# Attention's queries by seven block products in a stage of their own, in a one-core encoder block

## The chip, the cores and the metric

The kernel runs on one core of one Trainium2 chip. The metric is the device time of one execution in microseconds (us). TensorE (PE) multiplies matrices into PSUM (8 banks of 128 x 512 fp32), VectorE (DVE) and ScalarE (ACT) work on SBUF and PSUM, GpSimd (POOL) on SBUF alone. Transfers are started from SyncE's queue (SP), ScalarE's or GpSimd's; those from GpSimd can add into their destination. An engine works through its instructions in the order in which they are written down, and waits at each one until its inputs are there.

## The reference

One layer over T = 1040 positions (16 learned ones ahead of 1024), 1024 channels:

```
u = rms_norm(h);  z = u @ w_in                       # 7680 columns, cut into ten parts
o_r = bidirectional_retention(rot(rq), rot(rk), rv)  # 4 heads, chunks of 128, group norm
y_r = (o_r * silu(rg)) @ w_rb
o_a = windowed_attention(rot(aq), rot(ak), av, sink) # 8 heads in 2 groups, +-128 positions
y_a = (o_a * silu(ag)) @ w_ab
out = (sigmoid(gr) * y_r + sigmoid(ga) * y_a) @ w_o
return (h + rms_norm(out))[:, 16:]
```

The change is about aq = u @ w_in[aq], 1024 channels (8 heads of 128), and its rotation; and about which of the gates rg, ag, gr, ga are partly made early.

## The kernel before, in words

**Number format.** Every fp32 product is made of three matmuls in a faster format (mm3, lines 74 to 79): each operand is split into a high part h (a rounding copy, on ScalarE or GpSimd) and a low part l = value - h (dve_lo, line 91, on VectorE), and ah*bh + al*bh + ah*bl is accumulated in a PSUM bank. The input x, transposed and scaled by the norm's weights, lies in SBUF all the time as high and low part in two tiles named big (128 x 8 blocks x 1040).

**Stages.** (1) Setup, and a first projection. (2) Retention, head by head (retention): a forward pass over 9 chunks, then a backward pass over 8. The next head's query and key projection (gen_qk) is cut into steps of one mm3 per 128 channels and laid into the backward pass as a filler (fill(KT), 8 steps at a time); some gate products made ahead (gen_pre) follow. In the last head the filler is the first key group (gen_ak(0)), gate products and the first two query products (gen_aq(0, 0)). (3) The values' projection (gen_av, nine chunks). (4) Attention: 4 head pairs times 8 chunks of 128 queries. (5) The block phases z (gates), r, a (the two branch projections) and o (output projection).

**Seven products.** In the block phases a unit of 256 weight columns is taken as a 2 x 2 matrix of blocks (A11 to A22; 512 input channels by 128 columns) against x as a 2 x 2 matrix of blocks (B11 to B22; 512 channels by 512 positions). Seven products of sums of blocks, not eight of blocks, give the unit's four results (line 933 has the list: products 1 and 2 use A11*B11 and A12*B21, 3 uses B22, and 4, 5, 6, 7 use the sums T4, T1, T2, T3 of blocks of x). A product is 4 mm3 of 512 columns. T1 to T4 need space beside x; T1 takes the place of B12 in big, the last quarter of T4 that of the 16 learned positions. Phase.prepare forms and splits the weights' sums six products ahead (LEAD, line 1121); Phase.product multiplies; Phase.combine adds the results out of the PSUM banks; a post function finishes each result.

**The queries.** gen_aq (line 690) makes them the plain way: for each of 4 units, 2 column halves and 2 position halves, 8 mm3 of 512 columns. rope_late (line 180) rotates a result: two VectorE products out of PSUM (lines 184, 185), then two adding transfers from GpSimd's queue (line 187). split_q (line 661) splits it at a later step. Except for gen_aq(0, 0) all of it is filler in the attention.

**Attention.** For each chunk stage1 makes two score blocks, VectorE adds the mask and reduces (line 1423), ScalarE takes the exponential (line 1426), VectorE the reciprocal of the sum (line 1430), GpSimd scales (line 1439); stage2 transposes the weights (lines 1455 to 1460) and splits them; stage3 multiplies with the values (lines 76 to 78 and 1490). stage1 runs one chunk ahead. FILL (line 27) says how many filler steps a chunk gets, BEGUN (line 1547) what is done beside which filler step: weight fetches and splits, query splits, the sums of x for T1 to T4 (sum_fetch, sum_row), gates made ahead. tc.issue_after and follow lay an engine's instructions behind a named one; otherwise a planner orders each engine's instructions by its own estimate of when they are ready, and by their order in the program.

**Gates made ahead.** PRE (line 28) names, for gate units 2 to 13, the products whose x block is unchanged (2, and from unit 6 on 3); gen_pre makes them, stores them in DRAM (e_d), and the z phase adds them. So 20 of the z phase's 112 products are made earlier. Its first two units have an order of their own (early) that puts off T2 to T4, whose sums are read back from DRAM and split at its start (get_sum, line 1138).

Of the kernel before, what the change touches and what calls it, by code (L numbers as in the profile page):

```python
# [14 lines left out]
NM = 16  # L15
# [11 lines left out]
FILL = (9, 9, 7, 7, 7, 7, 6, 6), (7,) * 8, (7, 6, 6, 6, 6, 6, 6, 5), (5, 5, 5, 5, 5, 5, 8)  # L27
PRE = {u: (2, 3) if u > 5 else (2,) for u in range(2, 14)}
# [11 lines left out]
def block_kernel(ctx: ExitStack, tc: tile.TileContext, x0, xT, x, meta, w_in, w_rb, w_ab, w_out, post_w,  # L40
# [14 lines left out]
    def bank(tag, name):  # L55
# [12 lines left out]
    xs_d = [dram.tile([4, P, 2, 512], F32, tag=f"xs{i}", name=f"xs{i}") for i in range(2)]  # L68
    pre_d = {n: [dram.tile([P, 4, 512], F32, tag=f"pre{n}{s}", name=f"pre{n}{s}") for s in range(2)]
             for n in ("T1", "T2", "T3", "T4")}  # L70
# [354 lines left out]
    vah = va.tile([P, NB, 256], R, name="vah")  # L425
    vm = va.tile([P, 256], R, name="vm")
    vmt = va.tile([NM, 256], F32, name="vmt")
# [30 lines left out]
    def retention(h, fill, begin=lambda: None):  # L458
# [102 lines left out]
        for c in range(9):  # L561
# [7 lines left out]
            if h == NH - 1 and c == 1:  # L569
                pre_fetch(6)  # L570
            if h == NH - 1 and c == 2:
                with tc.issue_after(state["vl"]):
                    pre_sums(6)
# [10 lines left out]
            if h == 1 and c == 2:  # L584
                row_factors()
            stage2(c)
# [19 lines left out]
        for c in range(NB, 0, -1):  # L606
# [52 lines left out]
    aq, aqs, wq = {}, {}, {}  # L659

    def split_q(hp, e_, i):

        o = aq[hp][e_, i].rearrange("p (t q) -> p t q", q=64)
        if (hp, i) not in aqs:
            aqs[hp, i] = [aw.tile([P, 1024], R, tag=f"aq{t}", bufs=2, name=f"aq{t}{hp}_{i}") for t in "hl"], set()
            if len(aqs) == 1:
                aw.tile([P, 48], F32, name="space_aq")
        h, l = (t.rearrange("p (t e q) -> p t e q", e=2, q=64)[:, :, e_] for t in aqs[hp, i][0])
        nc.scalar.copy(h, o)
        dve_lo(l, o, h)  # L670
        aqs[hp, i][1].add(e_)


    def fetch_aq(hp):
        raw = fetch_w(w_in, U_AQ + hp)
        split, wq[hp] = halves_w(U_AQ + hp)
        begun["q", hp] = lambda s: split(raw[s], True)

    def fetch_ak():
        raw = fetch_w(w_in, U_AK)  # L680
        split, w_ = halves_w(U_AK)
        wak.append(w_)
        begun["k", 1] = lambda s: split(raw[s], True)

    def half_w(which, i, s):
        begun[which, i](s)

    begun = {}

    def gen_aq(hp, i, es=(0, 1)):  # L690
        if not i:
            if hp not in wq:
                wq[hp] = load_w(w_in, U_AQ + hp)
            aq[hp] = {}
        a, b = HALVES[i]
        for e_ in es:
            t = yield from proj(wq[hp], P * e_, a, b, f"paq{hp}_{i}{e_}")
            o = ra.tile([P, 512], F32, tag="q", bufs=6, name=f"aq{hp}_{i}{e_}")
            rope_late(t, a, b, o, f"aq{hp}_{i}{e_}")
            aq[hp][e_, i] = o  # L700
            yield
# [20 lines left out]
    def gen_ak(g, pieces_=range(4)):  # L722
        if not wak:
            wak.append(load_w(w_in, U_AK))
        for i in pieces_:
            a, b = PIECES[i]
# [3 lines left out]
            if not g and i:  # L730
                keys(g, i - 1)
            yield

    def last_keys():
# [3 lines left out]

    SUMS = ("T1", (0, 0), (0, 1), (0, 0)), ("T3", (0, 1), (1, 1), (0, 1)), ("T2", (1, 1), (1, 1), (0, 0)), (
        "T4", (1, 0), (1, 0), (1, 1))  # L740

    def sum_fetch(q):

        k, c = q // 2, slice(256 * (q % 2), 256 * (q % 2) + 256)
        for i in range(2):
            xsum[i] = t = ap.tile([P, 2, 256], F32, tag="xs", bufs=2, name=f"xs{i}{q}")
            nc.sync.dma_start(t, xT[4 * i + k, :, NM:T].rearrange("p (j t) -> p j t", j=2)[:, :, c])

    def sum_row(q, part):

        k, c = q // 2, slice(256 * (q % 2), 256 * (q % 2) + 256)
        if not part:
            for i, t in xsum.items():
                nc.scalar.activation(t, t, AF.Copy, scale=vec[:, 4 * i + k:4 * i + k + 1])
        x = {(i, j): t[:, j] for i, t in xsum.items() for j in range(2)}
        for _, o, a, b in SUMS[2 * part:2 * part + 2]:
            nc.vector.tensor_tensor(x[o], x[a], x[b], ALU.subtract)
        if part:
            for i, t in xsum.items():
                last["xs"] = nc.sync.dma_start(xs_d[i][k][:, :, c], t).ins  # L760

    xsum = {}
# [8 lines left out]
    def pre_split(k, i, behind):  # L771

        n, o, a, b = SUMS[i]
# [14 lines left out]
    def pre_fetch(u):  # L788
        n = P * len(PRE[u])
# [892 lines left out]
```

## Time and profile before

| | |
|---|---|
| median of 3 runs | 1041.22 us (1040.29 to 1041.6) |
| profiled execution | 1040.1 us, its span 1038.3 us |
| granted clock of TensorE | 0.999 |
| busy: TensorE, VectorE, ScalarE, GpSimd | 99%, 80%, 48%, 22% |
| TensorE instructions | 5883 matmuls, transposes included |
| query products (paq) | 384 matmuls, first at 288 us, last at 496 us |
| scores to last attention output | 332 to 550 us |
| z phase's products (bz) | 1104 matmuls, 546 to 803 us |
| moved by transfers | 188 MB, 181 GB/s on average |

The span is the time from the first to the last instruction; the execution's own time has 1.8 us more around it. A row of instructions reads: line, engine, operation, output<-inputs by tile names, shapes, count, then busy time in us and mean ns of one, then the engine's idle time just before them and what ended it. Matmuls overlap, so their shown durations add up to more than the time they take. A row of stage windows has the window, its length, each engine's busy us with the number of instructions, the granted clock, the transfer engines' share and GB/s.

### The profile page before, as it was taken

How to read it: one execution, taken by the hardware profiler on the slowest of the kernel's cores; microseconds unless marked ns; L12 is line 12 of the kernel's file. 1: busy time of each engine (PE TensorE's matmuls, PEld its weight loads, DVE VectorE, ACT ScalarE, POOL GpSimd, SP SyncE). 2: the span in 40 equal slices, each digit the busy share in tenths (PEclk: the TensorE clock that was granted, in tenths of full speed). 3: DMA queues.
4: the chain of work that ended last, by engine and by line, in shares of the span. 5: the costliest groups of instructions: out<-in, count | busy, mean ns of one | idle time of the engine just before them, and what ended most of it. 6: DMA issues, size and time to landing. Idle time of an engine off the chain costs nothing. (4 is left out here: it accounts for less than half of the span.)

```text
span 1038.3 us, 17311 instructions
## 1 busy us (share of the span) xinstructions
PE 1023.7 (99%) x5883; PEld 898.0 (86%) x5883; DVE 835.8 (80%) x1802; ACT 502.6 (48%) x1129; POOL 228.0 (22%) x368
## 2 busy tenths in 40 slices
PE   9999999999999999999999999999999999999997
PEld 8998999989989888988888888878888788788886
DVE  7886758768875778778769989999899799778665
ACT  5531432423424566665667554455567446334442
POOL 3445244243342333444310000000000000111032
PEclk9999999999999999999999999999999999999999
DMA  9433123243241466675559679899935746789464
GB/s 357 164 87 88 65 47 84 78 88 104 78 93 62 103 182 189 175 188 161 168 176 326 209 260 338 294 330 365 373 102 178 252 153 226 231 231 325 127 122 81
DMA packets 98840, 188.45 MB, mean 181 GB/s; under 512 B 13024, under 2 KB 37632, under 8 KB 98192
## 3 DMA queue, kind: packets, MB, share of 16 engines
q1 hardware_dynamic: 81200, 162.89, 46.6%
q0 software_dynamic: 10176, 14.73, 9.6%
q10 hardware_dynamic: 7376, 9.73, 2.7%
q8 instruction: 46, 0.75, 0.3%
q14 instruction: 42, 0.34, 0.1%
HBM read 124.32 MB, written 57.68 MB: 175 GB/s over the span
## 5 line engine op out<-in xcount | busy, mean ns | idle before, releaser
L1286 POOL DMA_DIRECT2D mx_d<-c1a x4 | 3.6, 890 | 395.8 <-DVE c1a L1277 377.2
L77 PE MATMUL bz<-big,llz 128*128 128x512 f32 x192 | 74.8, 390 | 0.2 <-DVE llz L92 0.2
L78 PE MATMUL bz<-big,lhz 128*128 128x512 f32 x192 | 74.4, 389 | 0.0
L76 PE MATMUL bz<-big,lhz 128*128 128x512 f32 x192 | 74.0, 390 | 0.3 <-ACT lhz L978 0.3
L76 PE MATMUL pv<-wh,big 128*128 128x256 f32 x256 | 72.8, 284 | 0.0
L77 PE MATMUL pv<-wh,big 128*128 128x256 f32 x256 | 72.7, 284 | 0.0
L78 PE MATMUL pv<-wl,big 128*128 128x256 f32 x256 | 72.7, 284 | 0.0
L76 PE MATMUL bz<-T,lhz 128*128 128x512 f32 x176 | 68.1, 390 | 1.1 <-DVE u2z L1068 1.1
L78 PE MATMUL bz<-T,lhz 128*128 128x512 f32 x176 | 68.5, 389 | 0.0
L77 PE MATMUL bz<-T,llz 128*128 128x512 f32 x176 | 68.5, 389 | 0.0
L76 PE MATMUL paq<-big,wh 128*128 128x512 f32 x128 | 51.6, 403 | 0.0
L1426 ACT ACTIVATE p<-raw,nm 128x337 f32<-128x337 f32 (+1 forms) x64 | 35.5, 556 | 32.2 <-DVE nm L1423 30.6
L77 PE MATMUL paq<-big,wl 128*128 128x512 f32 x128 | 50.2, 392 | 0.0
L78 PE MATMUL paq<-big,wh 128*128 128x512 f32 x128 | 50.2, 392 | 0.0
L1439 POOL TENSOR_SCALAR p<-p,den 128x336 f32<-128x336 f32 (+2 forms) x60 | 34.6, 624 | 66.5 <-DVE den L1430 59.1
L76 PEld LDWEIGHTS pv<-wh,big 128*128 128x128 f32 x256 | 48.3, 189 | 0.4
L77 PEld LDWEIGHTS pv<-wh,big 128*128 128x128 f32 x256 | 48.3, 189 | 0.4
L78 PEld LDWEIGHTS pv<-wl,big 128*128 128x128 f32 x256 | 48.2, 188 | 0.3
L92 DVE TENSOR_TENSOR wl<-wr,wh 128x1024 fp32r<-128x1024 f32 x28 | 35.1, 1258 | 10.4 <-POOL wh L89 6.7
L76 PEld LDWEIGHTS bz<-big,lhz 128*128 128x128 f32 x192 | 36.1, 188 | 8.1 <-ACT lhz L978 0.7
L77 PEld LDWEIGHTS bz<-big,llz 128*128 128x128 f32 x192 | 36.0, 188 | 7.9 <-DVE llz L92 0.5
L78 PEld LDWEIGHTS bz<-big,lhz 128*128 128x128 f32 x192 | 36.0, 188 | 7.5
(621 smaller groups left out, 3594.6 us busy)
## 6 DMA issues: line engine op xcount, KB each, us to landing
wrz<-in_w_in_dram SPq DMA_DIRECT2D x32, 512.0 KB, 6.1
wr<-in_w_in_dram SPq DMA_DIRECT2D x29, 512.0 KB, 4.1
we<-in_w_in_dram SPq DMA_DIRECT2D x16, 512.0 KB, 4.3
tg<-tg_d SPq DMA_DIRECT2D x32, 256.0 KB, 5.1
e<-e ACTq DMA_DIRECT2D x20, 256.0 KB, 2.7
e<-e SPq DMA_DIRECT2D x20, 256.0 KB, 5.3
xn<-in_x_dram SPq DMA_DIRECT2D x8, 512.0 KB, 9.5
oTr_d<-ost SPq DMA_DIRECT2D x16, 256.0 KB, 2.1
```

The source lines that it names most:

```text
L76: nc.tensor.matmul(o, ah, bh, start=first, stop=False, **kw)
L77: nc.tensor.matmul(o, al, bh, start=False, stop=False, **kw)
L78: latest[:] = [nc.tensor.matmul(o, ah, bl, start=False, stop=last, **kw).ins]
L92: return nc.vector.tensor_tensor(o, i, hi.bitcast(F32), ALU.subtract).ins
L1286: nc.gpsimd.dma_start(d, to, accum_op=ALU.add)
L1426: last["exp"] = nc.scalar.activation(pp[:, x_, w0 - o:w0 - o + 1 + wid], r[:, 0:1 + wid], AF.Exp, scale=-1.0, bias=nm_[:, x_:x_ + 1], accu ...
L1439: nc.gpsimd.tensor_scalar(v, v, den[:, x_:x_ + 1], 1.0, op0=ALU.mult, op1=ALU.mult)
```

## The change

- The queries get a stage of their own between the values and the attention: four units of 256 columns, each by seven block products, all eight PSUM banks. It needs T1 to T4 of x, so these are now made during the retention (row_sums, eight steps for each of four rows of blocks, one step at a chunk), split there, and stored in DRAM as high and low parts (xt_d). At the start of the query stage they are loaded in final form; T1 and T2 stay for the z phase, T3 and T4 are loaded again for it.
- A query result is rotated, split and stored in DRAM at once (q_post), from ScalarE's queue. The attention loads a head pair's half at a time (fetch_aq).
- At the two seams small pools hold what is needed first: the first products' weight parts lie in the rotation's buffers (m), the others in pools over retention's early buffers (qa, qt, qb); the attention's queries and gate operands lie in four pools in a row (aq, ep) over the place of T3.
- The second key group is made in the last retention head, in the place of the first queries, and waits in DRAM (ak_d). The values' low parts are put into DRAM during the query stage (val_d) and fetched back.
- The attention's filler is now the gates' products 5, 2 and 3 of units 8 to 15 alone (gen_gate): 96 steps, three for each chunk. Scores are made two chunks ahead, not one, with three weight buffers. GpSimd makes the gate operands' high parts (gate_part).
- The z phase runs its first two units in the usual order, and takes products 5, 2 and 3 of units 8 to 15 and product 2 of units 2 to 7 as made: 30 of 112. The sum for its product 6 comes from DRAM (s2_d). The next phase's operands are loaded and split from 25 products before its end on, not 16.

The core of the diff:

```diff
-FILL = (9, 9, 7, 7, 7, 7, 6, 6), (7,) * 8, (7, 6, 6, 6, 6, 6, 6, 5), (5, 5, 5, 5, 5, 5, 8)
-PRE = {u: (2, 3) if u > 5 else (2,) for u in range(2, 14)}
+PRE = {u: (2,) if u < 8 else (5, 2, 3) for u in range(2, 16)}
...
+    def row_sums(k):
+
+        x = va.tile([P, 2, 2, 512], F32, tag="vah", bufs=1, name=f"xs{k}")
+        with follow(asked[0]):
+            for i in range(2):
+                nc.sync.dma_start(x[:, i], xT[4 * i + k, :, NM:T].rearrange("p (j t) -> p j t", j=2))
+        yield
+        for i in range(2):
+            for j in range(2):
+                nc.scalar.activation(x[:, i, j], x[:, i, j], AF.Copy, scale=vec[:, 4 * i + k:4 * i + k + 1])
+            yield
...
+        def split(n):
+            o = x[:, *SUMS[n][0]]
+            h = va.tile([P, 512], R, tag="vm", bufs=1, name=f"xh{n}{k}")
+            nc.scalar.copy(h, o)
+            nc.sync.dma_start(xt_d[n][0][:, k], h.bitcast(F32))
+            with tc.issue_after(sums_at[0]):
+                dve_lo(o.bitcast(R), o, h)
+            nc.sync.dma_start(xt_d[n][1][:, k], o)
+
+        for ns, n in ((("T1", "T3"), None), ((), "T3"), (("T2",), "T1"), (("T4",), "T2"), ((), "T4")):
+            for m in ns:
+                minus(m)
+            if n:
+                split(n)
+            yield
...
     def retention(h, fill, begin=lambda: None):
...
+            if c > 1 and sums_at[0]:
+                sums_at[0] = state["vl"]
+                next(sums, None)
             stage2(c)
...
+            sums_at[0] = near
+            if h or c < 8:
+                next(sums, None)
...
+    def fetch_aq(n):
+
+        hp, i = n // 2, n % 2
+        aqs[hp, i] = [aqp[i].tile([P, 1024], R, tag=f"aq{t}", bufs=1, name=f"aq{t}{hp}_{i}") for t in "hl"]
+        for e_ in range(2):
+            for t, d in zip(aqs[hp, i], aq_d[hp, e_, i]):
+                nc.sync.dma_start(t.bitcast(F32).rearrange("p (t e q) -> p t e q", e=2, q=64)[:, :, e_],
+                                  d.rearrange("p (t q) -> p t q", q=64))
...
-                 [gen_ak(0), pieces(pre, 8), last_keys(), gen_aq(0, 0)])
+                 [gen_ak(0), pieces(pre, 8), last_keys(), gen_ak(1)])
...
+    def gate_part(u, p):
+
+        a11, a21, a12, a22 = (t[:, :, P * i:P * i + P] for t in raw[u] for i in range(2))
+        g = nc.vector.tensor_tensor
+        if p == 5:
+            g(a21, a21, a22, ALU.add)
+        if p == 3:
+            g(a11, a21, a11, ALU.subtract)
+            nc.sync.dma_start(s2_d[u], a11)
+            g(a22, a12, a11, ALU.subtract)
+        src = {5: a21, 2: a12, 3: a22}[p]
+        m = (3 * (u - 8) + (5, 2, 3).index(p)) // 2 % 2
+        h, l = (epp[m].tile([P, 4, P], R, tag=f"e{x_}", bufs=2, name=f"e{x_}{u}_{p}") for x_ in "hl")
+        pool_hi(h, src)
+        dve_lo(l, src, h)
+        parts[u, p] = h, l
...
+    def q_post(u, i, j, o, to=None):
+        to = o if to is None else to
+        a, b = HALVES[j]
+        rope_late(o, a, b, to, f"aq{u}_{i}{j}")
+        h = ra.tile([P, 512], R, tag="m", bufs=4, name=f"aqh{u}_{i}{j}")
+        nc.scalar.copy(h, to)
+        nc.scalar.dma_start(aq_d[u, i, j][0], h.bitcast(F32))
+        dve_lo(to.bitcast(R), to, h)
+        nc.scalar.dma_start(aq_d[u, i, j][1], to)
...
+    free[:] = ["pj"] * 3 + ["p1"] * 2 + ["p2"] * 2 + ["p3"]
+    q_seq = [(0, 1), (0, 2), (1, 1), (1, 2)] + [(e_, p) for p in (5, 6, 7, 3, 4) for e_ in range(2)]
+    q_seq += [(2 + e_, p) for p in (1, 2, 5, 6, 7, 3, 4) for e_ in range(2)]
+    q_steps = run([(Phase("q", q_seq, w_loader(w_in, range(U_AQ, U_AQ + 4)), q_post), None)])
+    next(q_steps)
+    with follow(*raw_asked):
+        for n in ("T1", "T2", "T3", "T4"):
+            get_pre(n, xt_d)
+    for _ in q_steps:
+        pass
+    free[:] = ["pj"] * 3
+    for i, t in enumerate(val):
+        val[i] = ra.tile([P, 512], R, tag="q", bufs=6, name=f"val{i}b")
+        nc.sync.dma_start(val[i].bitcast(F32), val_d[i])
...
         for k, (hp, n) in enumerate(chunks):
             ends = k >= len(chunks) - 2
-            if k + 1 < len(chunks):
+            if k + 2 < len(chunks):
                 with follow(*latest, *marks("oa", "lo")):
-                    stage1(*chunks[k + 1])
+                    stage1(*chunks[k + 2])
+                with follow(*latest):
+                    fill(1)
...
             with follow(*latest, *marks("exp", "sum")) if not ends else ExitStack():
                 stage2(hp, n)
             if not ends:
                 with follow(*latest):
-                    fill(FILL[hp][n] if k else 1)
+                    fill(2)
```

More of the change, by code (lines that the diff above doesn't have):

```diff
@@ L657, in filler @@
         return fill, drain
[L659 to L701, printed above, removed]
+    aqs = {}
+    def fetch_aq(n):
[5 more added lines that the diff above has]
+                                  d.rearrange("p (t q) -> p t q", q=64))
     kT = {}
@@ new lines, in gen_pre @@
+    def gen_pre(u):
+        t = keep.tile([P, 4, 256], F32, tag="wr", bufs=2, name=f"we{u}")[:, :, 0:P]
+        nc.sync.dma_start(t, w_in[gates[u], :, 4:8, 0:P])
+        h, l = (wp.tile([P, 4, 256], R, tag=f"w{x_}", bufs=4, name=f"we{x_}{u}")[:, :, 0:P] for x_ in "hl")
+        nc.scalar.copy(h, t)
+        dve_lo(l, t, h)
+        b = pj(f"pe{u}")
+        for k in range(4):
+            mm3(b, h[:, k], l[:, k], xh[4 + k][:, NM:NM + 512], xl[4 + k][:, NM:NM + 512], k == 0, k == 3, True)
+            if k < 3:
+                yield
+        made(u, 2, b)
+        yield
@@ L1006, in prepare @@
                 g(t, t, self.block(u, "A11"), sub)
+            elif p == 6 and 3 in known:
+                t = half("S2")
+                nc.sync.dma_start(t, s2_d[u])
+                self.split(u, 6, t)
             elif p == 6:
@@ L1361, in block_kernel @@
     ph_o = Phase("o", seq, o_load, o_post, apart=(0, 1))
[L1362 to L1363 removed]
+    steps = run([(Phase("z", sequence(16), w_loader(w_in, gates, PRE), z_post, z_fetch, late=(0, 1), pre=PRE),
                   act_src(oTr_d)),
```

408 lines of the change are left out of this document (197 added, 211 removed).

## The prediction, made before the result was known

> **What bounds the kernel now.** I read the page's busy times first, then stage windows, then the waits of TensorE, then single timelines.
>
> ```profile
> span 1038.3 us, 17311 instructions
> PE 1023.7 (99%) x5883; PEld 898.0 (86%) x5883; DVE 835.8 (80%) x1802; ACT 502.6 (48%) x1129; POOL 228.0 (22%) x368
> ```
> ```profile
> core 0: us, PE busy (x) PEld busy (x) DVE busy (x) ACT busy (x) POOL busy (x), PEclk, DMA share, GB/s
> 66.00:290.00 224.00, 224.00 (x1691) 212.46 (x1690) 168.44 (x453) 74.85 (x219) 90.35 (x136) 1.00 0.33 83
> 331.00:545.00 214.00, 211.65 (x1276) 187.56 (x1275) 161.82 (x426) 129.99 (x351) 74.21 (x156) 1.00 0.59 164
> 545.00:797.00 252.00, 250.41 (x1111) 206.76 (x1110) 234.27 (x387) 142.80 (x255) 0.00 (x0) 1.00 0.81 279
> 700.00:750.00 50.00, 50.00 (x222) 41.37 (x221) 43.09 (x70) 26.48 (x46) 0.00 (x0) 1.00 1.03 375
> ```
> ```profile
> PE idle L313 <- DVE warm L207: 1.4, 1, 1.4
> PE bz L76 <- DVE u2z L1068: 1.1, 1, 1.1
> ```
>
> TensorE is never idle in the retention (66 to 290 us), idle 2.35 us of 214 in the attention and 1.6 us of 252 in the z phase. Its longest wait is 1.4 us, at the start. So nothing but fewer matmuls can shorten this kernel by much, and every new wait of TensorE lengthens it. VectorE is the runner-up: 75% in the retention, 76% in the attention, 93% in the z phase, and at 93% TensorE lost only those 1.6 us.
>
> **What a matmul costs.** Matmuls overlap, so a price is a distance between starts.
>
> ```profile
> 401.37 0.40 PE L77 MATMUL paq<-big,wl 128*128 128x512 f32 x1
> ...
> 405.73 0.40 PE L78 MATMUL paq<-big,wh 128*128 128x512 f32 x1
> ```
> ```profile
> 0.00:1038.00 1038.00, 252.17 (x1104) 206.95 (x1104) 42.16 (x62) 23.30 (x40) 1.00 0.59 182
> ```
>
> The first fence is the start and end of twenty query matmuls in a row in the attention: 19 steps in 4.36 us, 0.2295 us each, though each is shown with 0.40 us. The second is the z phase's block products alone (tile bz, over the whole run): 1104 matmuls of the same shape in 252.17 us, 0.2284 us each. By the shown durations a dropped matmul would seem to be worth 0.39 us; that would nearly double the gain.
>
> [...]
>
> **The change, part by part.**
>
> *Matmuls.* Now: 4 weight units, 2 column halves, 2 token halves, 8 blocks, 3 matmuls: 384. After: 4 units, 7 products, 4 blocks, 3: 336. That removes 48 x 0.2295 = 11.0 us, and the other 336 run at the z phase's pace, 336 x 0.0011 = 0.4 us. The gates' products stay 112 in all: 20 were made ahead, now 30, so the z phase has 82 instead of 92. The second key group moves from the attention into the last retention head, in the place of the first queries. Their numbers don't change. **Gain 11.4 us.**
>
> *Attention's old waits.* Its 2.35 us of idle time belong to a schedule that goes. I take them off (2.3) and cost the new schedule whole.
>
> *Sums in the retention.* Each of four rows now brings 4 scalings and 4 high copies on ScalarE, 4 subtractions and 4 low parts on VectorE, 8 stores and 2 loads on SP's queue. The z row gives 234.27 us for 387 VectorE instructions, mostly of this shape: 0.605 us each. 32 of them are 19.4 us; VectorE goes from 75% to 84% of the stage. Nothing is queued behind the new instructions but the scan itself (state update, its split, the next state product). Bounds: 0, if they fall in idle time, and 19.4, if each delays the scan in full; no gain, since it only adds work. The nearest row is the z phase, 93% with 1.6 us lost: I take **1 us**.
>
> *Seam from values to queries.* The first four products use B11 and B21, which lie ready, and their weight parts use an early pool. A product is 12 x 0.2284 = 2.74 us, so T1 has 11.0 us from the stage's start, T2 16.4, T3 21.9.
>
> ```profile
> T<-preT SPq DMA_DIRECT2D x4, 1024.0 KB, 8.8
> aq<-m_aq POOLq DMA_DIRECT2D x32, 128.0 KB, 4.0
> ```
>
> A pair of such loads lands in 8.8 us. T1 overwrites x, so it can't start before the last value chunk has read its first four blocks, half a chunk ahead of the stage. It is then about 3 us early. On SP's queue the last value store and two units' weights stand ahead of it, T2 to T4 behind it at up to 375 GB/s (window 700 to 750): 2 MB each 5.6 us, as fast as pairs of products use them. Bounds 0 and 8.8 us (nothing overlaps); I take **1 us**.
>
> *The query stage.* VectorE per unit: 7 low parts, 4 sums of weights, 3 additions, and for each of 4 results two rotary products and one low part: 26, so 104 in all, 104 x 0.605 = 63 us beside 28 x 2.74 = 76.7 us of TensorE. ScalarE has 14 copies a unit. Both fit. What is new is the order: each of 16 results goes VectorE, two accumulating transfers from POOL's queue (4.0 us to land), ScalarE's copy, VectorE's low part, two stores from ScalarE's queue. If a low part stands in VectorE's queue before its transfer has landed, the next product's weight parts are queued behind it. The stores' waits hold only ScalarE, which is half idle. Operands are made six products (16 us) ahead, which hides single waits. Bounds: 0, and 16 x 4.0 - 13.7 (VectorE's spare time) = 50 us. Before, the same parts were made at a hand-set later step, so the trace doesn't show the case; nearest is again the z phase's 1.6 us: **1.5 us**.
>
> *Seam from queries to attention.* The first query pair comes back from DRAM when T3 is done with, four products (11 us) before the end; the values come back into the products' own buffers; the gate operands need T3's place too. The first softmax has four filler steps and two score products to hide in. Bounds: 0, and 9 us (four loads at 4.0 to 5 us, then a 4 us softmax, all bare); **1 us**.
>
> *The attention.* It loses most of its filler: three steps a chunk instead of about seven, with scores made two chunks ahead.
>
> ```profile
> 405.96 0.28 PE L76 MATMUL po<-pah,vah 128*128 128x256 f32 x1
> ...
> 406.77 0.32 PE L76 MATMUL ps<-kTh,aqh 128*128 128x336 f32 x1
> ...
> 407.43 0.57 DVE L1423 CUSTOM_DVE_ANT_0 raw<-ps,mask,nsink 128x336 f32<-128x336 f32 x1
> ...
> 407.69 0.60 PE L1455 MATMUL pt<-ident,p 128*128 128x128 f32 x4
> ...
> 408.37 0.47 PE L76 MATMUL paq<-big,wh 128*128 128x512 f32 x1
> ...
> 408.69 0.39 PE L77 MATMUL paq<-big,wl 128*128 128x512 f32 x1
> ...
> 409.37 0.17 DVE L1430 RECIPROCAL den<-den 128x2 f32<-128x2 f32 x1 [0.87 <-ACT p L1426]
> ...
> 411.59 1.22 DVE L92 TENSOR_TENSOR wl<-wr,wh 128x1024 fp32r<-128x1024 f32 x1
> ```
>
> TensorE: scores 406.77 to 407.69, 0.92; transposes to 408.37, 0.68; output 0.81 for a chunk of 7 matmuls, so 1.16 for the usual 10; filler 9 x 0.2295 = 2.07, and 0.09 more after the transposes (408.37 to 408.69). Together 4.92 us. VectorE: from the first score reduction (407.43) to where it is free again (411.59) 4.16 us, 0.87 of it waiting for ScalarE's exponentials; plus 48 gate instructions over 32 chunks, 1.5 x 0.605 = 0.91: 5.07 us if none falls into a wait. So the chunk is bound by TensorE by 0.76 us without gates, or by VectorE by 0.15 us with all of them serial: 0 to 4.8 us over 32 chunks. If ScalarE's copies of gate results (three in four chunks) also come ahead of the copy that VectorE waits for:
>
> ```profile
> L835 ACT COPY e<-pe 128x512 f32<-128x512 f32 x20 | 11.7, 588 | 18.4 <-PE pe L78 17.8 <-DMA wrz<-in_w_in_dram 0.6
> ```
>
> 0.75 x 0.588 = 0.44 more a chunk, up to 18.9 us in all. Most gate low parts wait for POOL's high part and can slip into the 0.87: I take **2 us**.
>
> *The z phase.* It drops 16 splits of x sums at its start and recomputes no fourth sum; T1, T2 lie ready, T3 and T4 have eight products to come. Per product it has no more VectorE work than before, so its 1.6 us stay and I cost it at nothing; without that cover T3's 8.8 us would lie open.
>
> **Sum.** The profiled execution took 1040.1 us (span 1038.3). 1040.1 - 11.4 - 2.3 + 1.0 + 1.0 + 1.5 + 1.0 + 2.0 = 1032.9. The median shown is 1.1 above the profiled execution, and I carry that over: **1034.0 us**, 0.7% less.
>
> **Rivals.**
>
> *All covers hold.* No new wait: 1040.1 - 13.7 + 1.1 = 1027.5, up to 1029.5. For it: TensorE loses nothing in the retention at 75% VectorE. Against it: three new seams. Chance 0.20.
>
> *T1 comes late.* If 3 MB stand ahead of it (8 us at 375 GB/s), TensorE waits 4 to 6 us instead of 1: about 1039. Chance 0.07. [...]
>
> *The attention becomes VectorE's.* The chain serial with ScalarE's copies in it: 9 to 18.9 us instead of 2, 1041 to 1051, nearer the first since the waits take up some. For it: 5.07 against 4.92. Against it: 0.87 us of waits in each chunk that gate parts can use. Chance 0.11; a third of it slower.
>
> *VectorE waits for the rotary transfers (slower).* The place is the low part behind the accumulating transfer in the query stage. Its price is 16 w - 13.7 for a wait of w each; it outweighs the whole saving from 16 w - 13.7 > 8.7, w > 1.4 us. With half the transfer's 4.0 us, w = 2: 18.3 us instead of 1.5, 1050.8. For it: weights, sums, queries and rotary parts are some 24 MB in 77 us, 313 GB/s, close to the 375 at which the engines are full, so transfers lengthen. Against it: 16 us of lead. Chance 0.15.
>
> **Chances.** Forecast (1029.5 to 1039) 0.47. A measurement here can tell about 0.2%: faster is below 1039.1, slower above 1043.3. Faster: 0.47 + 0.20 + 0.05 (T1 late but small) + 0.01 = 0.73. Same: 0.02 + 0.06 = 0.08. Slower: 0.04 + 0.15 = 0.19. Range: from 1027, no new wait, to 1045, which leaves most of the last rival and half of the slow attention out, near 0.2.
>
> **What would show it.** 5835 matmul instructions instead of 5883. Query products at 0.228 us from start to start over some 77 us without a break. In the waits of TensorE: under 2 us each by T1, by query operands and by attention transposes. VectorE near 84% in the retention with TensorE still full. Attention chunks of 4.9 to 5.0 us. I am wrong if query operands' low parts end TensorE's waits for over 5 us, if chunks take 5.2 us or more, or if a gap of over 3 us stands at a seam.

## The result and the profile after

The changed kernel takes **1107.06 us** (median of 4 runs, 1106.21 to 1109.97), the kernel before 1041.08 (4 runs, 1040.29 to 1041.6). The ratio is 1.064, with a 95% interval from 1.0619 to 1.066. The forecast was 1034.0 us with a range up to 1045, so it was wrong in its sign and by 73 us. The profiled execution took 1107.45 us, its span 1105.7.

The page of the changed kernel: busy time and share of each engine with its number of instructions, then two rows of the 40 slices (27.6 us each).

```profile
span 1105.7 us, 17586 instructions
...
PE 1032.2 (93%) x5835; PEld 898.0 (81%) x5835; DVE 841.4 (76%) x1812; ACT 501.0 (45%) x1133; POOL 246.7 (22%) x394
...
PE   9899999999999967449999999999999999999997
...
PEclk9999999999999997869999999999999999999999
```

The matmuls are the 5835 of the forecast. TensorE's busy time has gone up although 48 matmuls are gone: where the granted clock is low, each takes longer (a 128x512 matmul is shown with 0.63 us from 421.50 to 426 us, with 0.39 from 428.50 on). Both dips stand in slices 15 to 18, 387 to 498 us.

TensorE's three longest waits in the changed kernel (line waited for, then total, number, longest):

```profile
PE pe L79 <- ACT e L779: 23.8, 1, 23.8
PE bq L79 <- ACT u2q L1080: 15.4, 2, 15.2
PE ps L79 <- DVE nm L1482: 7.2, 4, 2.6
```

Before, the longest was 1.4 us. The two long ones name ScalarE, an engine that is busy 45% of the time. Its stages, by window:

```profile
core 0: us, PE busy (x) PEld busy (x) DVE busy (x) ACT busy (x) POOL busy (x), PEclk, DMA share, GB/s
66.00:290.00 224.00, 220.17 (x1652) 206.96 (x1651) 174.83 (x469) 88.72 (x245) 86.79 (x126) 1.00 0.45 127
345.00:440.00 95.00, 79.58 (x336) 64.51 (x336) 55.78 (x98) 27.66 (x48) 17.77 (x22) 0.91 0.76 227
440.00:490.00 50.00, 18.98 (x87) 15.35 (x86) 24.46 (x56) 13.61 (x35) 18.21 (x31) 0.73 0.75 200
```

In the query stage (345 to 440 us) and at attention's start (440 to 490) no engine is full: TensorE 84% and 38%, VectorE 59% and 49%, ScalarE 29% and 27%, the transfers 76% and 75%. Where nothing is full on average, the order of the steps is the first suspect. The retention has 39 matmuls fewer in its window than before (1652 against 1691).

The stages' lengths in us, each from the start of its first matmul (values pav, queries bq, scores ps, gates bz) in the profiled executions, with three of the experiments beside them (before, the values are followed by the attention at once):

| | before | after | e2 | c1 | c2 |
|---|---|---|---|---|---|
| start to values | 301.4 | 315.9 | 316.5 | 309.0 | 309.6 |
| values | 30.4 | 28.9 | 29.3 | 29.1 | 30.0 |
| query stage | - | 95.3 | 78.0 | 78.5 | 77.8 |
| attention | 214.2 | 194.0 | 175.6 | 181.7 | 174.0 |
| z phase to the end | 492.3 | 471.6 | 471.4 | 471.7 | 472.0 |

**The chain in the query stage.** Timelines of the changed kernel from 402 us on (start, length, and in brackets the idle time just before and what ended it): VectorE, GpSimd's queue, ScalarE.

```profile
402.02 0.69 DVE L188 TENSOR_TENSOR u2q<-u2q,cr 128x512 f32<-128x512 f32 x1
...
404.29 0.69 DVE L187 TENSOR_TENSOR m_aq<-u2q,sr 128x512 f32<-128x512 f32 x1
410.05 0.69 DVE L95 TENSOR_TENSOR u2q<-u2q,aqh 128x512 fp32r<-128x512 f32 x1 [5.07 <-ACT aqh L1398]
410.66 0.68 DVE L188 TENSOR_TENSOR u2q<-u2q,cr 128x512 f32<-128x512 f32 x1
```
```profile
403.00 1.64 POOL L190 DMA_DIRECT2D u2q<-m_aq  x2 [4.41 <-DVE u2q L188]
411.64 1.64 POOL L190 DMA_DIRECT2D u2q<-m_aq  x2 [7.00 <-DVE u2q L188]
```
```profile
409.40 0.62 ACT L1398 CAST aqh<-u2q 128x512 fp32r<-128x512 f32 x1 [5.75 <-DMA u2q<-m_aq]
...
415.48 0.62 ACT L1398 CAST aqh<-u2q 128x512 fp32r<-128x512 f32 x1 [4.94 <-DMA u2q<-m_aq]
...
419.75 0.62 ACT L1398 CAST aqh<-c5q 128x512 fp32r<-128x512 f32 x1 [3.66 <-DMA c5q<-m_aq]
420.28 0.58 ACT L1080 COPY u2q<-bq 128x512 f32<-128x512 f32 x1
```

On VectorE the sine product of post i+1 (404.29) stands ahead of post i's low part (410.05), but its cosine product (410.66) stands behind it. The low part waits for ScalarE's high copy (409.40), that one for the transfers asked for at 403.00. So post i+1 can send its transfers only when post i's have landed. This order holds for 11 of the 15 pairs of neighbouring posts; in the other four both products of the next post stand ahead of the low part. The first high copy starts at 376.80 us and the last at 482.76, 15 distances of 7.06 us on average: 8.2 us in the 11 interlocked pairs, 3.9 in the other four. 76.7 us for 16 posts would allow 4.8. TensorE feels it by way of ScalarE: the copy of product 6 out of its bank (420.28), which has to be made before the next product adds to the same bank, is queued behind high copies that wait for transfers, 5.75, 4.94 and 3.66 us. They make up most of the 15.2 us. The 23.8 us are the same thing with the last posts and the first gate copy (ScalarE):

```profile
467.36 0.62 ACT L1398 CAST aqh<-u2q 128x512 fp32r<-128x512 f32 x1 [5.00 <-DMA u2q<-m_aq]
...
482.76 0.62 ACT L1398 CAST aqh<-c5q 128x512 fp32r<-128x512 f32 x1 [5.80 <-DMA c5q<-m_aq]
483.28 0.58 ACT L779 COPY e<-pe 128x512 f32<-128x512 f32 x1
```

**The start.** SyncE's queue and ScalarE in the changed kernel:

```profile
12.79 1.80 SPq L1616 DMA_DIRECT2D out_dram<-in_x_dram  x2
15.42 0.34 SPq L110 DMA_DIRECT2D wr<-in_w_in_dram  x1
16.63 0.51 SPq L1616 DMA_DIRECT2D out_dram<-in_x_dram  x1
17.96 0.33 SPq L110 DMA_DIRECT2D wr<-in_w_in_dram  x1
```
```profile
28.26 1.05 ACT L121 CAST wh<-wr 128x1024 fp32r<-128x1024 f32 x1 [9.18 <-DMA wr<-in_w_in_dram]
32.02 1.04 ACT L121 CAST wh<-wr 128x1024 fp32r<-128x1024 f32 x1 [2.71 <-DMA wr<-in_w_in_dram]
```

Three copies of 1 MB from x to the output, meant for the attention, go out in the first 17 us, ahead of weights that the retention's first products (tile pv) need. In the kernel before they went out at 429, 442 and 489 us. The change had tied them to an instruction of ScalarE (`last["oa"]`) where the kernel before tied them to one of SyncE (`last["xs"]`), and that tie holds back nothing on SyncE's queue.

### The profile page after: what moved, and what is told of

It is laid out like the page before. It is cut to its first block, busy times and chain, and to the rows that moved or that the text cites. A ratio compares the mean times of both kernels' runs of the same rounds, so it can differ in the third digit from the quotient of the medians.

```text
span 1105.7 us, 17586 instructions
## 1 busy us (share of the span) xinstructions
PE 1032.2 (93%) x5835; PEld 898.0 (81%) x5835; DVE 841.4 (76%) x1812; ACT 501.0 (45%) x1133; POOL 246.7 (22%) x394
## 5 line engine op out<-in xcount | busy, mean ns | idle before, releaser
L79 PE MATMUL pe<-big,eh 128*128 128x512 f32 x96 | 41.5, 432 | 27.6 <-ACT e L779 23.8
L80 PE MATMUL bz<-big,llz 128*128 128x512 f32 x152 | 59.2, 389 | 0.0
L79 PE MATMUL bz<-big,lhz 128*128 128x512 f32 x152 | 58.5, 390 | 0.8 <-ACT lhz L988 0.8
L81 PE MATMUL bz<-big,lhz 128*128 128x512 f32 x152 | 59.1, 389 | 0.0
L79 PE MATMUL bz<-T,lhz 128*128 128x512 f32 x112 | 43.9, 392 | 2.2 <-DVE u2z L1083 1.3
L80 PE MATMUL bz<-T,llz 128*128 128x512 f32 x112 | 43.6, 389 | 0.0
L81 PE MATMUL bz<-T,lhz 128*128 128x512 f32 x112 | 43.4, 389 | 0.0
L79 PEld LDWEIGHTS pe<-big,eh 128*128 128x128 f32 x96 | 18.6, 194 | 30.5 <-ACT e L779 24.0
L80 PE MATMUL pe<-big,el 128*128 128x512 f32 x96 | 38.9, 405 | 1.0 <-DVE el L95 1.0
L1482 DVE CUSTOM_DVE_ANT_0 raw<-ps,mask,nsink 128x336 f32<-128x336 f32 (+2 forms) x60 | 31.2, 548 | 10.2 <-PE ps L81 9.3
L81 PE MATMUL pe<-big,eh 128*128 128x512 f32 x96 | 38.8, 404 | 0.0
L95 DVE TENSOR_TENSOR wl<-wr,wh 128x1024 fp32r<-128x1024 f32 x18 | 22.7, 1263 | 17.5 <-ACT wh L121 10.2
L639 ACT ACTIVATE ost<-to,rnw 128x128 f32<-128x128 f32 x64 | 19.9, 366 | 35.2 <-PE to L634 31.0
## 6 DMA issues: line engine op xcount, KB each, us to landing
xn<-in_x_dram SPq DMA_DIRECT2D x8, 512.0 KB, 10.4
```

What stands on the lines that cost most here:

```text
L79: nc.tensor.matmul(o, ah, bh, start=first, stop=False, **kw)
L80: nc.tensor.matmul(o, al, bh, start=False, stop=False, **kw)
L81: latest[:] = [nc.tensor.matmul(o, ah, bl, start=False, stop=last, **kw).ins]
L95: return nc.vector.tensor_tensor(o, i, hi.bitcast(F32), ALU.subtract).ins
L639: nc.scalar.activation(ost[0][:, e_, w0:w0 + P], to[:, P * e_:P * e_ + P], AF.Copy, scale=rnw[:, 2 * h + e_:2 * h + e_ + 1])
L1482: nc.vector.tensor_tensor_reduce(r[:, o:o + wid], s[:, 0:wid], seen, -SCALE, nsink[:, hp:hp + 1], ALU.add, ALU.min, nm_[:, x_:x_ + 1])
```

## The experiments

Medians of 4 runs each; the kernel before took 1040.2 to 1040.7 us beside them.

**e1, the copies of x behind a load on SyncE's queue.**

```diff
-        with tc.issue_after(last["oa"]):
+        with tc.issue_after(last["sp"]):
             nc.sync.dma_start(out[P * r:P * r + 2 * P], x[P * r:P * r + 2 * P])
```

Here `last["sp"]` is the newest load of fetch_aq.

> One edit: the three copies of x into the output are queued behind a load on SyncE's own queue, so they cannot start before attention. Theory (these 3 MB go out at 13 to 17 us ahead of the value weights, which makes the weights' high copies 5 to 8 us late and costs TensorE three waits and 3.4 us of half clock at 29 to 38 us): the first product of the values comes 6 us earlier after the start, no half-clock stretch at 34 us, 1107 - 6 = 1101 us (1099 to 1103). Rival (the start is late because the sums' buffers or the engines' order changed, not because of the copies): 1105 to 1109 us, and the waits at 29 to 33 us stay.

Measured: 1097.64 us, 9.4 less. The values start at 309.4 us, 6.5 earlier. TensorE's waits for the weights of the first products (tile pv; 0.90, 1.50 and 0.94 us at 30 to 35 us in the changed kernel, with a granted clock of 0.57 from 34 to 38) are no longer in its list, and the mean granted clock is 0.980 instead of 0.974. The weights are now asked for at 12.57 us in one go (SyncE's queue of e1):

```profile
12.57 3.51 SPq L110 DMA_DIRECT2D wr<-in_w_in_dram  x2
```

So the copies were the cause of these 6.5 us, of 14.5 that the values start later than before the change; another 3 us came out of the stages behind them, and why stays open.

**e2, the second half of each post two posts later.**

```diff
...
+        crs = rope_late(o, a, b, to, f"aq{u}_{i}{j}")
+        def finish():
+            h = ra.tile([P, 512], R, tag="m", bufs=4, name=f"aqh{u}_{i}{j}")
+            nc.scalar.copy(h, to)
+            nc.scalar.dma_start(aq_d[u, i, j][0], h.bitcast(F32))
+            dve_lo(to.bitcast(R), to, h)
+            nc.scalar.dma_start(aq_d[u, i, j][1], to)
+        unfinished.append(finish)
+        if len(unfinished) > 2:
+            with follow(crs, *marks("copy")):
+                unfinished.pop(0)()
```

`crs` is the newest post's cosine product on VectorE, "copy" the newest bank copy on ScalarE. The last two are finished after the stage.

> One edit: the second half of each query post (high copy, stores, low part) is written two posts later, so that on VectorE both products of the next two posts stand ahead of the low part that waits for the transfers, and on ScalarE the high copy stands behind the bank copies. Theory (each post's chain of product, transfer, high copy and low part is strung out one after another by the engines' order, 6 to 7 us a post against 4.8 that a post may take): posts 3 to 5 us apart, the waits of 15.2 and 23.8 us shrink to under 8 together, 1107 - 33 = 1074 us (1066 to 1084). Rival A (the accumulating transfers themselves are the rate, GpSimd's issues and landings one after another): posts stay over 6 us apart, 1103 to 1110 us. Rival B (only the late weights of the second pair matter): the posts of the first pair still start at 377 us and the gain is under 8 us.

Measured: 1076.31 us, 30.8 less. The two waits of 15.2 and 23.8 us are down to 0.2 and 8.5, a little over the 8 that were expected. The first high copy is no earlier (379.42 us), but the 15 distances are 4.60 us each. The query stage takes 78.0 us, and TensorE is full in it (windows of e2); of its waits from 345 to 490 us these two are the longest:

```profile
346.00:424.00 78.00, 77.17 (x337) 62.64 (x336) 59.51 (x104) 28.32 (x50) 23.08 (x28) 1.00 0.99 287
424.00:450.00 26.00, 13.21 (x61) 10.12 (x62) 16.72 (x44) 11.09 (x31) 12.98 (x24) 0.81 1.04 258
```
```profile
PE pe L79 <- ACT e L780: 8.5, 1, 8.5
PE ps L79 <- DVE nm L1494: 1.8, 2, 1.5
```

Rival B falls with the size of the gain. Rival A, the transfers as the rate, falls too: the transfers of a post even got slower. Median time from issue to landing, first in the changed kernel, then in e2 (tile u3q, where it grew most):

```profile
u3q<-m_aq POOLq DMA_DIRECT2D x8, 128.0 KB, 3.7
```
```profile
u3q<-m_aq POOLq DMA_DIRECT2D x8, 128.0 KB, 6.2
```

By tile a transfer takes 1.3 to 2.5 us longer, with the transfer engines' share at 0.99 of the query stage instead of 0.76, and the kernel is 31 us faster. The length of a transfer was not the price; standing in line behind it was.

**e3, the rotation without transfers.**

```diff
...
+        for r in (0, 64):
+            nc.vector.tensor_tensor(m[64 - r:128 - r, 0:n], t[r:r + 64, 0:n], sr[r:r + 64, a:b], ALU.mult)
+        nc.vector.tensor_tensor(o[:, 0:n], t[:, 0:n], cr[:, a:b], ALU.mult)
+        nc.gpsimd.tensor_tensor(o[:, 0:n], o[:, 0:n], m[:, 0:n], ALU.add)
```

> One edit: the query posts turn their halves with two 64-partition products on VectorE and one addition on GpSimd; their 32 accumulating transfers are gone. 16 more VectorE products, 16 more GpSimd additions. Theory (the wait for the transfers, standing in VectorE's and ScalarE's queues, is what made the query stage long): the waits of 15.2 and 23.8 us and the half-clock stretches behind them go, the stage from the values to attention takes 80 to 85 us instead of 95, 1107 - 45 = 1062 us (1055 to 1070). Rival A (VectorE's own work is the bound of the stage): the stage stays at 90 us or more and the 16 added products show, 1095 us or more. Rival B (the late weights of the second pair): high copies still start at 377 us or later, gain under 15 us.

Measured: 1084.10 us, 23.0 less instead of 45. Windows of e3:

```profile
390.00:405.00 15.00, 15.00 (x68) 12.43 (x67) 14.88 (x22) 5.74 (x10) 2.97 (x2) 1.00 0.31 106
405.00:420.00 15.00, 13.65 (x60) 10.77 (x59) 14.86 (x21) 5.61 (x10) 4.00 (x3) 1.00 0.26 82
```

VectorE is busy 99% of these 30 us: each post costs it one more instruction of 0.7 us and the posts stay 6.7 us apart. TensorE loses only 1.35 us in the same 30, so the price comes later: from 431 to 450 us it is busy 10.4 of 19 us, with a wait of 4.6 us for VectorE, and at attention's start one of 6.1 us for GpSimd. The query stage takes 88.9 us. Rival A, VectorE's work as the bound, fits the half of the gain that is missing; that VectorE's full stretch causes the later waits is read from this and from e6, not followed wait by wait.

**e6, e2 and e3 together** (the halves turned as in e3, the second half of a post two posts later).

> The edits of e2_deferred and e3_no_transfers together (the rotation on the engines, the second halves two posts later). e3_no_transfers gave back 23 us where 45 were expected, with VectorE busy 14.9 of 15 us in the middle of the stage. Theory (VectorE's own work is then the bound, 16 more products): putting the second halves later changes little, 1078 to 1086 us, VectorE again over 95% busy from 390 to 430 us. Rival (the strung-out order was still the bound): as good as e2_deferred or better, 1068 to 1076 us.

Measured: 1083.53 us, as e3, with VectorE at 14.80 and 14.82 of 15 us in the same two windows. So with the rotation on the engines the order no longer matters, which speaks for VectorE's work. The transfers in the change are right as such: e2 and e6 differ only in how the rotation is done, and e2 is 7.2 us faster.

**e4, no rotation.**

```diff
-        rope_late(o, a, b, to, f"aq{u}_{i}{j}")
+        nc.vector.tensor_tensor(to[:, 0:512], o[:, 0:512], cr[:, a:b], ALU.mult)
```

> Work left out: the query posts' rotation; a post is one product with the cosine table, the high copy, the low part and the two stores. It gives a floor for what the rotation costs in this stage. Theory of the transfers: 1058 us (1050 to 1066), at most 8 us under the run with the rotation on the engines alone. Rival (weights, loads and stores of the stage are the bound, rotation or not): the stage still takes over 88 us and the time stays above 1090.

Measured: 1071.42 us. It missed the theory's bound of 1066, and was 12.7 us under e3, where at most 8 were expected; the rival's 1090 is far off. The posts are still 5.01 us apart, though their chain holds no transfer any more, and e2 with all its transfers is better by the stage: 78.0 us against 84. TensorE's longest waits in it are 4.7 us for the gate weights' high part and 3.5 us for a bank copy; neither was tried apart. The edit leaves out one VectorE product for each post as well as the transfers.

**c1, e1 and e2 together.**

> The edits of e1_copies and e2_deferred together. Theory (two causes in two places, the start and the query stage, that have nothing to do with each other): the gains add, 1107.1 - 9.4 - 30.8 = 1067 us (1064 to 1070). Rival (the late start had been hiding some of the wait in the query stage, or the copies put into attention jam it): 1071 us or more.

Measured: 1072.01 us, so the gains don't add: 4.3 us less than e2 instead of 9.4. The table shows where it went: the values start 7.5 us earlier, and attention is 6.1 us longer. It makes the loss look larger than the medians do, since e2's profiled execution (1072.86 us) was the shortest of its four. The copies do not fill this place: in c1 they go out at 494 and 535 us. VectorE in c1:

```profile
418.13 0.68 DVE L188 TENSOR_TENSOR u2q<-u2q,cr 128x512 f32<-128x512 f32 x1
424.96 0.69 DVE L187 TENSOR_TENSOR m_aq<-bq,sr 128x512 f32<-128x512 f32 x1 [6.14 <-DMA u2q<-m_aq]
```

The last posts come one upon another, and the rotation's four buffers (m) are held by transfers that land late just then (the wait of 6.14 us above is for one, with the transfer engines' share at 0.91 from 416 to 455 us). VectorE stands still for 6.1 us, and with it the second score block's reduction, which is queued behind it; TensorE waits as long for the bank that this post's products empty. In e2 VectorE's wait at the same place was 2.9 us. Why it is longer in c1 was not tried.

**c2, and the last two posts' second halves inside attention.**

```diff
+        with follow(*marks("exp", "sum", "made")):
+            unfinished.pop(0)()
```

One stands after attention's second filler steps and one in chunk 0, each behind the newest exponential, reciprocal and gate copy.

> As c1_copies_deferred, and the second halves of the last two posts are put behind attention's first exponentials and the first gate copy on ScalarE. Theory (after e2_deferred TensorE still waits 8.5 us for a gate copy that stands on ScalarE's queue behind the last posts' high copies, and that wait brings half clock): the 8.5 us and the half clock behind it go, 1067 - 9 = 1058 us (1055 to 1062). Rival (the seam is bound by something else, VectorE's last posts or the value tiles that are reloaded into their buffers): 1064 us or more, with another wait of 5 us or more between 420 and 450 us.

Measured: 1066.00 us, 6.0 less than c1 where 9 were expected. The 8.5 us are gone, and part of them comes back as another wait, as the rival says (waits of c2):

```profile
PE pe L79 <- POOL eh L92: 7.2, 4, 5.7
PE pt L1524 <- DVE pal L95: 2.5, 1, 2.5
```

**e5, a quarter of the sums.**

```diff
-        for k in range(4):
-            yield from row_sums(k)
+        yield from row_sums(0)
```

> As c1_copies_deferred, but work is left out: only the first of the four quarters of the eight sums is formed during retention, its parts are stored four times. Theory (of the 7 us that retention is longer than before, the sums' products and copies on VectorE and ScalarE are the cause): the values start 5 us earlier than in c1_copies_deferred, 1067 - 5 = 1062 us (1060 to 1064). Rival (retention is longer because of the other order of the fills or the tiles' places): within 1.5 us of c1_copies_deferred.

Measured: 1063.07 us, 8.9 less than c1. The values start at 303.9 us, 5.1 earlier, as the theory says. From 40 to 300 us c1's TensorE has these waits; e5's and the first kernel's lists are empty there:

```profile
PE pkv L79 <- ACT khf L543: 0.9, 3, 0.4
PE pkv L80 <- DVE klf L544: 0.5, 1, 0.5
PE pa L80 <- DVE sl L95: 0.5, 1, 0.5
PE tr L530 <- DVE sd L552: 0.4, 1, 0.4
```

They are steps of the retention's scan; with two of 0.3 us they add up to 2.9 of the 5.1 us, and the rest is not in this view. Three quarters of the sums cost 5.1 us up to the values, so all four some 6.8, an estimate by proportion. e5 leaves out three quarters of the rows' loads too; which part of a row costs how much was not taken apart.

**e7 and c3, the last six posts turned on the engines as in e3** (rope_turn), on top of c1 and of c2.

```diff
-        crs = rope_late(o, a, b, to, f"aq{u}_{i}{j}")
+        crs = (rope_turn if u > 1 and i + j else rope_late)(o, a, b, to, f"aq{u}_{i}{j}")
```

> As c1_copies_deferred, and the last six query posts turn their halves on the engines instead of by accumulating transfers (12 transfers of 128 KB less, 6 more VectorE products, 6 GpSimd additions). In c1 the start came 7 us earlier but 5 of them went again at the seam to attention, where VectorE waits 6.1 us for a buffer of the rotation that a transfer holds while the DMA engines are full. Theory (the four small rotation buffers, each held through a slow transfer, are what bounds the seam): that wait goes and half-clock stretches with it, 1072 - 6 = 1066 us (1062 to 1069). Rival (VectorE's work or the gate copy on ScalarE takes its place, 8.5 us in c1): 1070 to 1076 us.

> As c2_last_posts_late, and the last six posts turned on the engines as in e7. Theory (with the transfers and the gate copy's place both out of the way the seam is bound by the loads that all come there at once): the wait for the gate weights' high parts, 5.7 us in c2, shrinks a little because 1.5 MB of transfers are gone, 1066 - 4 = 1062 us (1058 to 1064). Rival (VectorE, with more products at the seam, is the bound): 1066 to 1072 us. Neither expects less than the kernel before, 1041 us: the sums in retention and the shorter cover behind the gates remain.

Measured: e7 1067.61 us, 4.4 less than c1, within the theory's range; c3 1069.28 us (1065.89 to 1070.68), no better than c2 (1064.31 to 1068.82), as its rival says. In both, VectorE is busy 29.7 and 29.5 of the 39 us from 416 to 455 us, against 20.1 in c1. By stages (profiled executions) c3's attention is 2.1 us shorter than c2's and its query stage 4.5 us longer: what is won at the seam is lost before it, where VectorE has more to do. That VectorE's work is the cause is argued from its busy time alone.

**e8, the stores back on SyncE's queue.**

```diff
-        nc.scalar.dma_start(aq_d[u, i, j][0], h.bitcast(F32))
+        nc.sync.dma_start(aq_d[u, i, j][0], h.bitcast(F32))
...
-        nc.scalar.dma_start(aq_d[u, i, j][1], to)
+        nc.sync.dma_start(aq_d[u, i, j][1], to)
```

> One edit to the changed kernel: the 32 query stores go back from ScalarE's queue to SyncE's. Theory (the stores' place is not what bounds the stage, the strung-out chain is): 1107 us, 1102 to 1112. Rival A (the stores' issues of 0.33 us or more on ScalarE make the high copies late): 1095 us or less. Rival B (stores that wait for posts stand ahead of the fetched queries and gate weights on SyncE's queue): 1115 us or more.

Measured: 1107.28 us. The stores' queue makes no difference.

**e9, the first high copies ahead of the second pair's weights on ScalarE.**

```diff
-            nc.scalar.copy(h, src)
+            with follow(*marks("aqh")) if self.nm == "q" and u > 1 and p == 1 else ExitStack():
+                nc.scalar.copy(h, src)
```

> One edit to the changed kernel: on ScalarE the high copies of the second pair's first weights are put behind the high copies of the posts that were written before them. In the changed kernel the first post's high copy waits 20 us behind a weights' copy whose load had not come. Theory (posts then still run at 6 to 7 us each, but the string starts 13 us earlier, so it ends earlier): first high copy at about 363 us, posts done about 470 us instead of 484, 1107 - 11 = 1096 us (1090 to 1101). Rival (the string is not started by that copy: its place in the queue was harmless): 1104 us or more.

Measured: 1102.72 us (1098.04 to 1106.24), 4.3 less, between the two and hardly clear of that spread. The reading of the 20 us was wrong. ScalarE in e9:

```profile
374.46 0.59 ACT L1081 COPY u3q<-bq 128x512 f32<-128x512 f32 x1 [1.68 <-PE bq L81]
374.94 0.62 ACT L1399 CAST aqh<-c1q 128x512 fp32r<-128x512 f32 x1
```

With the weights out of the way the first high copy starts 1.9 us earlier; it stood behind the bank copies of a later product as well. The string started late by the whole order, not by one load.

**e10, c2 without the rotation (the edit of e4), and e11, c2 with the gate weights first:**

```diff
         gate_part(8, 2)
+        gate_part(8, 3)
+        gate_fetch(9)
         stage1(0, 0)
```

> As c2_last_posts_late, but work is left out: a post's rotation is one product with the cosine table, without transfers. Theory (after the order is mended the rotation's transfers hide, and what is left of the loss at attention's start comes from the loads and gate parts that meet there): 1063 us (1059 to 1067). Rival (the transfers, landing late while the DMA engines are full, still hold the seam): 1056 us or less, and the wait for the gate weights' high part falls under 2 us.

> As c2_last_posts_late, and the first gate unit's third weight part is formed, and the second gate unit's weights are asked for, before attention's first chunk instead of inside it. Theory (SyncE asks for those weights only at 432 us, when their buffer comes free, so the high part comes 5.7 us late and half clock follows): the wait goes, 1066 - 7 = 1059 us (1055 to 1062). Rival (the next thing in the row, value tiles or VectorE's extra work ahead of the first softmax, takes its place): 1064 us or more.

Measured: e10 1060.95 us, 5 under c2 and inside the theory's range, with the wait for the gate weights as long as ever (6.5 us). e11 1066.53 us: no wait for them over 1.2 us is left and others take its place, as the rival says (its longest waits from 417 to 456 us):

```profile
PE ps L79 <- DVE nm L1492: 3.7, 2, 2.2
PE pe L79 <- ACT e L780: 3.4, 1, 3.4
```

So some 5 us belong to the rotation even in the best order; e10 leaves out its transfers and one VectorE product for each post together, so they are not told apart. No single wait holds the rest of attention's start, and what bounds it stays open.

No version beats the kernel before. c2 and e11, the best that compute everything, take 2.5% and 2.4% more (1.0224 to 1.0269 and 1.0209 to 1.0268).

## Why the prediction was wrong

*Matmuls*: right. 5835 of them; 984 matmuls of gate products in the z phase; c2's query stage of 77.8 us against 76.7 worked out.

*The query stage* is the step that failed. It gave 1.5 us, on three reasons. "Operands are made six products (16 us) ahead" holds for weight parts, but not for the copy that empties a bank, which can't be made ahead and shared ScalarE's queue with the high copies. "The stores' waits hold only ScalarE, which is half idle" took a share of busy time for freedom: an engine that works in order is blocked by the one instruction at its head (ScalarE for 5.75, 4.94 and 3.66 us by a high copy at 409 to 420 us). And the 4.0 us of a transfer were set against VectorE's spare time, as if each post waited once; because product, transfer, high copy and low part of neighbouring posts were interlocked, 11 of the 15 pairs of posts went in single file, and the posts came 7.06 us apart instead of 4.8. 15 x 2.26 = 34 us; undoing the interlock gave 30.8 (e2). The rival "VectorE waits for the rotary transfers" had the place and the sign, but looked for the damage in the next product's weight parts: none of TensorE's waits in the list of this stage names one, the long one names ScalarE's bank copy. Its formula gives the 34 us with w = 3, a value fitted afterwards; I took w = 2 and a chance of 0.15. Of the prediction's own signs of being wrong, a gap of over 3 us at a seam came (23.8 us), long waits for query operands' low parts did not.

*Sums in the retention*: the mechanism was right, the size was not. I took 1 us, near the lower end, since the z phase lost only 1.6 us at 93% of VectorE; it is about 7 (e5, by proportion), with VectorE at 78% of the window and not the 84% worked out. The share says how full the engine is; the waits that e5 removes are steps of the scan, in front of which the new instructions stand.

*The start* was not in the sum at all: the working does not mention the three copies, whose tie had moved from an instruction of SyncE to one of ScalarE. 6.5 us at the start, 9.4 in all (e1).

*Seam from values to queries*: right; TensorE is idle for 0.2 us of the 29 from 316 to 345 us.

*Seam from queries to attention*: 1.0 us given. Attention takes 194.0 us, where 32 chunks of 4.92 are 157 and its first and last steps some more; 20.0 us of the difference are gone in c2. The upper bound of 9 us counted loads and a softmax; the posts that were still unfinished were not among them.

*The attention* once it runs: right. From one chunk's output copy to the next, 20 of 31 distances in the changed kernel lie between 4.4 and 5.0 us, with a mean of 5.06, so it did not become VectorE's.

*The z phase*: nothing given. It lost its 10 products of 2.74 us, but is 20.7 us shorter, not 27.4. A wait of 2.0 us for a low part stands where the next phase begins, with half clock behind it (0.66 on average from 856 to 861 us). TensorE's waits in the z phase and at this step come to 5.2 us, against 2.4 before; with the 1.7 us that the half clock costs, this is 4.5 of the missing 6.7 us. It was not tried apart; that fewer products leave less time to form the next phase's operands is only argued.

## What to carry to other kernels

Where an engine works in order, ask of each wait that you add what is queued behind it, and do so for the half idle engine too: a copy that frees a bank, behind a copy that waits for a transfer, stops the busiest engine of all (TensorE for 15.2 us here). A chain that crosses several engines should have its later half written some steps behind its first half; then a slower transfer costs far less: in e2 the transfers are slower and the kernel 31 us faster, though e10 shows that the rotation still costs some 5 us. When a gain of 1% rests on a full TensorE, look for every instruction whose tie or place changes, also the ones that the change doesn't speak of.

## What was not expected of the hardware

TensorE's clock fell after some short waits. At the end of the z phase in the changed kernel:

```profile
856.36 0.50 PE L80 MATMUL br<-big,llr 128*128 128x512 f32 x1 [1.96 <-DVE llr L95]
...
857.50 0.63 PE L80 MATMUL br<-big,llr 128*128 128x512 f32 x1
857.92 0.63 PE L81 MATMUL br<-big,lhr 128*128 128x512 f32 x1
...
860.34 0.39 PE L81 MATMUL br<-big,lhr 128*128 128x512 f32 x1
860.57 0.39 PE L79 MATMUL bz<-T,lhz 128*128 128x512 f32 x1
```

After a wait of 1.96 us the matmuls start 0.42 us apart instead of 0.23, for about 3.4 us (856.70 to 860.06). The granted clock is 0.66 from 856 to 861 us, which costs another 1.7 us. The forecast has no term for such a stretch.

The length of the wait alone does not decide whether one follows. The same wait of 1.96 us in e1 has no slow stretch behind it; the matmuls there are shown with 0.40 and 0.39 us:

```profile
845.54 0.50 PE L80 MATMUL br<-big,llr 128*128 128x512 f32 x1 [1.96 <-DVE llr L95]
845.88 0.40 PE L81 MATMUL br<-big,lhr 128*128 128x512 f32 x1
...
847.94 0.39 PE L81 MATMUL br<-big,lhr 128*128 128x512 f32 x1
```

In the changed kernel itself a wait of 2.60 us (until 452.30) has full clock behind it, too (1.00 from 452.3 to 456 us). What else decides it stays open. In the changed kernel the half clock makes the two longest waits dearer: the granted clock is 0.50 behind that of 15.2 us (421.5 to 426.2 us) and behind that of 23.8 us (484 to 488 us), and 0.73 from 440 to 490 us.
